# Two output projections and the embedding gate: 512 output channels per product, weights by half of the contraction, one open sum per token tile

## The chip, the cores and the metric

The kernel runs on one core of a Trainium2 chip. The metric is the device time of one execution in microseconds, median of the timed runs: 1736.26 us before the change (three runs, 1733.51 to 1736.67). The engines are called PE (matrix products), PEld (PE's weight loads), DVE (VectorE), ACT (ScalarE), POOL (GpSimd) and SP (which issues most DMAs).

## The reference, cut to what matters

Two transformer-like blocks on 512 tokens of 1024 channels. The three products that the change touches are `w_out` (block 1), `w_out_2` and `w_ple_gate_2` (block 2), each 512 x 1024 times 1024 x 1024:

```
merged = sigmoid(g_attn) * a + sigmoid(g_conv) * s
x = x + g1 * einsum('btd,de->bte', merged, w_out)            # block 1
...
hx2 = modulate(rmsnorm(x, norm2_g), sh2, sc2)
logits = hx2 @ w_router; affinity = softmax(logits)          # top 64 tokens of each of 16 experts
x = x + g2 * experts(...)                                    # 16 experts, three 1024 x 1024 matrices each
...
x = x + m @ w_out_2                                          # block 2
x = x + sigmoid(rmsnorm(x) @ w_ple_gate_2) * (p @ w_ple_2)   # embedding gate
out = rmsnorm(x) * final_g
```

## The kernel before, in words

Every large product is done in float32r in three parts (`mm3`: high times high, high times low, low times high; both operands are split beforehand into a high part, on ACT, and the rest, on DVE). Weights come through the class `Weights` in the order of use: a chunk of 8 x 128 rows and 256 columns is loaded by SP into tag `wr` (two buffers) and split into `wh` and `wl` (two buffers each). Loading chunk i+2 is queued when the split of chunk i begins.

The three products concerned have tokens on the output's partitions (`gemm_tc`): the token tile of the activations (128 x 128) is stationary and 256 columns of the weights move. For 512 output columns the kernel takes two chunks at once, and goes through the four token tiles one after the other: 2 chunks x 8 steps of the contraction x 3 products for a tile, then that tile's sum is complete and its follow-up work is issued. There are two such passes (512 columns each) per product, so 2 x 4 x 48 = 384 products of 256 columns for each of the three.

The order of all engines is the order in which the Python code issues instructions; each engine works through its own queue in that order. Follow-up work is placed with `hooks` at numbered steps of a tile's products.

- First projection (`gemm_x1`, activations `mg`): after a tile, `post_x1` multiplies by the gate and adds x (DVE, two passes); one tile later `half_T` transposes the rows on PE, copies them and sums their squares on ACT, and in the second pass computes the norm on DVE and POOL; `half_mm` multiplies by the router and computes the softmax (a row of small DVE operations `lg`, `mx`, `aff` around one ACT exponential); `router_aff(t)` transposes tile t's affinities. After the last tile come `router_aff(2)`, `half_T(3, 1)`, `half_mm(3, 1)` and `router_aff(3)`, and then the choice of the top 64, a chain on DVE alone. `eload(tags)` loads the next pieces of the experts' weights into the buffers of the tags named; a piece that has been used calls `eload` with its own tag for the next one, so the first list of tags sets which buffers the pieces of all experts use. At the end of the experts the buffers of tag `wr` go to the first two chunks of block 2.
- Second projection (`post_x3`, activations `m2`): DVE adds the tile to the residual rows `acc`, ACT sums its squares. `norm3(t)` (DVE, POOL power, two DVE passes) makes the normalized rows `x3r`, `put_x3(t)` transposes them (eight PE transposes) and splits them into `x4` (two ACT copies `x4h`, two DVE subtractions `x4l`).
- Embedding gate (activations `x4`): `post_x4` is a sigmoid on ACT, a multiplication and an addition on DVE, a sum of squares on ACT. In the second pass `finish(t)` follows: DVE sum, POOL power, a scaling on DVE of one half and on ACT of the other, and the output's DMAs. The last tile is cut in two pieces of 256 columns.

Of the kernel before, what the change touches and what calls it, by code (L numbers as in the profile page):

```python
# [35 lines left out]
def _constants():  # L36
    """Tables that follow from the shapes alone."""
# [25 lines left out]
def tile_two_blocks(ctx: ExitStack, tc: tile.TileContext, a, out):  # L63
# [41 lines left out]
    # ------------------------------------------------------------------ first loads  # L105
# [78 lines left out]
    # ------------------------------------------------------------------ weights  # L184
# [3 lines left out]
    def warm(n):  # L188
        """products with zeros that keep TensorE's clock up where it would wait for others"""
# [3 lines left out]

    class Weights:
        """Chunks of 256 columns in the order of use: loaded ahead, split exactly into two float32r parts."""

        def __init__(self, specs, allocs=None):
            self.allocs = {} if allocs is None else allocs
# [12 lines left out]
        def begin(self):  # L211
            """the next chunk to be split, after those taken as they are"""
# [10 lines left out]
            if kind in self.allocs:  # L223
                hi, lo = self.allocs[kind](sh)
            else:
                hi = wp.tile([128] + sh, F32R, name="wh", tag="wh")
                lo = wp.tile([128] + sh, F32R, name="wl", tag="wl")
# [4 lines left out]
        def steps(self, i, n=4, lo_engine=None):  # L232
            """split of chunk i (or of the next one that is to be split) in 2 n steps, of ScalarE and VectorE in turn"""
# [31 lines left out]
    class Split:  # L265
        """[128, k, n] as two float32r parts, in buffers of 8 KiB"""
# [23 lines left out]
    def gemm_ct(ps, w, m, xs, nk=KT):  # L290
        """ps[ch, tok] = w[:, m-th 128 columns].T @ xs"""
# [6 lines left out]
    def gemm_tc(ps, w, t, xs, nk=KT):  # L298
        """ps[tok, ch] = xs[:, t-th 128 tokens].T @ w"""
# [62 lines left out]
    # ------------------------------------------------------------------ modulation, norms of x and ctx  # L362
# [38 lines left out]
    def unit(t0, between=lambda: None):  # L401
        """rows of two tiles over their root mean square"""
# [24 lines left out]
    specs += [(w_o1, 0), (w_o1, 256, "b2"), (w_o1, 512), (w_o1, 768, "b2")]  # L427
    wallocs = {}
    W = Weights(specs, wallocs)
# [54 lines left out]
    # keys and values, their products by parts of the contraction as these become known: several sums  # L484
    # are open in a bank, and a product with zeros starts them all
# [107 lines left out]
    def rope(ps, t0):  # L593
        """rotary embedding: [128 tokens, 2 tiles, 4 heads * 64] in PSUM -> [128, 2, 4, 64] in SBUF"""
# [15 lines left out]
    # ------------------------------------------------------------------ keys and values  # L610
# [44 lines left out]
    # steps of a chunk before the split of the next one begins  # L655
# [35 lines left out]
    def ct_chunk(xs, post, hooks=None):  # L691
        """256 channels [ch, tok], two PSUM tiles, each passed to post(m, psum)"""
# [11 lines left out]

    def mod256(n, pool):
        """columns 2048 + 256 n of the modulation"""
# [41 lines left out]
            # columns of the scores in PSUM: own keys before the context's, after them in the last block  # L748
# [105 lines left out]
    # ------------------------------------------------------------------ gated merge  # L854
# [16 lines left out]
    def spread(dst, cols_, tmp_):  # L871
        """columns [128, 8] as a row of 1024 on every partition"""
# [23 lines left out]
    wallocs["b2"] = lambda sh: (big2("wbh", sh, F32R), big2("wbl", sh, F32R))  # L896
# [4 lines left out]
    for j in range(4):  # L901
# [15 lines left out]
        for q, (xs, post) in enumerate(((hx, gate), (os_, proj_a), (hx, gate), (ys_, proj_c))):  # L917
# [7 lines left out]
            if j == 3 and q == 3:  # L925
                i0 = ci[0] + 1
                hooks = {14: [lambda: W.split(i0 + 1)]}
# [3 lines left out]
    # ------------------------------------------------------------------ output projection, router  # L931
# [17 lines left out]
    def router_prep():  # L949
        """the shift's part of the logits on every partition; the gain goes into the weights"""  # L950
# [16 lines left out]
    def post_x1(t, s_, pv):  # L967
        """x + gate * projection"""
# [42 lines left out]
    # the last pair's by halves of the columns, the very last rows in smaller pieces  # L1011
# [55 lines left out]
    def gemm_x1(t, n, ws, hooks):  # L1067
# [4 lines left out]
        for c in range(2):  # L1072
            p_ = bank() if cut or not c else p_
            for _ in gemm_tc(p_[:, c * 256:c * 256 + 256], ws[c], t, mg):
                for h in hooks.get(st, ()):
                    h()
# [810 lines left out]
```

## Time and profile before

| what | value |
|---|---|
| timed runs | 1733.51, 1736.26, 1736.67 us |
| span of the profiled execution, first to last instruction | 1732.3 us |
| PE busy | 1689.4 us (98%) |
| DVE, ACT, POOL busy | 893.1, 590.8, 65.9 us |
| mean granted clock of PE | 0.994 |
| first projection, first to last product | 585.3 to 644.1 us |
| second projection | 1628.4 to about 1676 us |
| embedding gate, first product to the end | 1676.9 to 1732.3 us |

The page lists the profiled execution by its span alone; the median of the timed runs is 3.96 us above that span. "Busy" on PE includes the time in which one product overlaps the next, so the distance from start to start of two products, not the duration of one, tells what one more costs.

### The profile page before, as it was taken

How to read it: one execution, taken by the hardware profiler on the slowest of the kernel's cores; microseconds unless marked ns; L12 is line 12 of the kernel's file. 1: busy time of each engine (PE TensorE's matmuls, PEld its weight loads, DVE VectorE, ACT ScalarE, POOL GpSimd, SP SyncE). 2: the span in 40 equal slices, each digit the busy share in tenths (PEclk: the TensorE clock that was granted, in tenths of full speed). 3: DMA queues.
4: the chain of work that ended last, by engine and by line, in shares of the span. 5: the costliest groups of instructions: out<-in, count | busy, mean ns of one | idle time of the engine just before them, and what ended most of it. 6: DMA issues, size and time to landing. Idle time of an engine off the chain costs nothing.

```text
span 1732.3 us, 23047 instructions
## 1 busy us (share of the span) xinstructions
PE 1689.4 (98%) x9500; PEld 1214.4 (70%) x9500; DVE 893.1 (52%) x1646; ACT 590.8 (34%) x1133; POOL 65.9 (4%) x68
## 2 busy tenths in 40 slices
PE   8999999999999999999999999979999999999998
PEld 5987777777778895443444344347898888877898
DVE  4655565565433433112211221276889999955544
ACT  5454545445322322110111011142435443354333
POOL 2000000000000000000000000040000010000000
PEclk9999999999999999999999999999999999999999
DMA  9243333331222668999999999942332222233431
GB/s 335 90 137 98 98 98 98 119 120 55 97 86 92 223 272 325 361 402 409 409 409 409 409 409 409 400 135 74 97 98 81 90 94 86 88 122 98 131 113 49
DMA packets 176217, 334.56 MB, mean 193 GB/s; under 512 B 6925, under 2 KB 120370, under 8 KB 175856
## 3 DMA queue, kind: packets, MB, share of 16 engines
q1 hardware_dynamic: 173712, 328.50, 52.2%
q0 software_dynamic: 1024, 2.37, 0.4%
q10 hardware_dynamic: 1376, 2.23, 0.4%
q8 instruction: 74, 1.21, 0.3%
q14 instruction: 31, 0.25, 0.0%
HBM read 328.88 MB, written 4.19 MB: 192 GB/s over the span
## 4 chain that ended last, share of the span: by engine, by line
PE 91%; DVE 5%; DMA 2%; ACT 1%; issue 1%; SPq 0%; POOL 0%; POOLq 0%; ACTq 0%; DVEq 0%
PE pb L286 15%; PE pb L287 15%; PE pb L288 15%; PE pu L1204 6%; PE py L1204 6%; PE pg L1168 4%; PE po L806 2%; PE pT L798 2%; PE pb L379 1%; PE s L767 1%; PE pg L1225 1%; DMA wr<-w_in 1%; PE pq L286 1%; PE pq L288 1%; PE pq L287 1%
## 5 line engine op out<-in xcount | busy, mean ns | idle before, releaser
L245 DVE TENSOR_TENSOR wl<-wr,wh 128x512 fp32r<-128x512 f32 x316 | 226.0, 732 | 120.7 <-ACT wh L247 120.7
L247 ACT ACTIVATE wh<-wr 128x512 fp32r<-128x512 f32 x320 | 183.6, 620 | 89.2 <-PE pb L287 63.7
L1559 DVE SCALAR_TENSOR_TENSOR co<-cin,cols,co 128x512 f32<-128x512 f32 x240 | 188.5, 785 | 4.1
L286 PE MATMUL pb<-h2h,wh 128*128 128x512 f32 x448 | 177.3, 396 | 0.0
L287 PE MATMUL pb<-h2l,wh 128*128 128x512 f32 x448 | 174.8, 390 | 0.0
L288 PE MATMUL pb<-h2h,wl 128*128 128x512 f32 x448 | 174.6, 390 | 0.0
L286 PE MATMUL pb<-hxh,wh 128*128 128x512 f32 x320 | 130.3, 407 | 0.0
L288 PE MATMUL pb<-hxh,wl 128*128 128x512 f32 x320 | 125.4, 392 | 0.0
L287 PE MATMUL pb<-hxl,wh 128*128 128x512 f32 x320 | 125.3, 391 | 0.0
L1204 PE MATMUL pu<-ew,xe 128*64 128x512 f32 x512 | 114.8, 595 | 0.0
L1204 PE MATMUL py<-ew,hb 128*64 128x512 f32 x440 | 101.0, 597 | 0.0
L286 PEld LDWEIGHTS pb<-h2h,wh 128*128 128x128 f32 x448 | 84.4, 188 | 19.6 <-issue 2.2
L288 PEld LDWEIGHTS pb<-h2h,wl 128*128 128x128 f32 x448 | 84.2, 188 | 17.9
L287 PEld LDWEIGHTS pb<-h2l,wh 128*128 128x128 f32 x448 | 84.3, 188 | 17.3 <-issue 0.5
L1239 DVE SCALAR_TENSOR_TENSOR yt<-py,gt__5984,g2b 128x512 f32<-128x512 f32 x15 | 10.6, 747 | 144.8 <-PE py L1204 138.3
L773 DVE CUSTOM_DVE_ANT_0 P<-s,cst,sink 128x512 f32<-128x512 f32 (+1 forms) x64 | 52.2, 816 | 57.9 <-PE s L770 57.9
L1204 PEld LDWEIGHTS pu<-ew,xe 128*64 128x64 f32 x512 | 35.3, 137 | 66.0 <-issue 65.4
L1171 ACT ACTIVATE xe<-pg,modc,ga 128x128 f32<-128x128 f32 x64 | 25.9, 454 | 147.8 <-PE pg L1168 147.8
L1168 PEld LDWEIGHTS pg<-Gs,xr 128*128 128x128 f32 x512 | 61.1, 196 | 21.5 <-issue 19.5
L777 ACT ACTIVATE P<-P,m 128x512 f32<-128x512 f32 (+1 forms) x64 | 49.8, 777 | 75.3 <-DVE m L776 70.3
L288 PEld LDWEIGHTS pb<-hxh,wl 128*128 128x128 f32 x320 | 60.0, 188 | 13.3
L286 PEld LDWEIGHTS pb<-hxh,wh 128*128 128x128 f32 x320 | 60.2, 188 | 12.4 <-issue 3.2
(457 smaller groups left out, 3294.6 us busy)
## 6 DMA issues: line engine op xcount, KB each, us to landing
ew<-w_exp_gate SPq DMA_DIRECT2D x64, 1024.0 KB, 17.3
ew<-w_exp_up SPq DMA_DIRECT2D x64, 1024.0 KB, 14.1
ew<-w_exp_down SPq DMA_DIRECT2D x59, 1024.0 KB, 16.1
wr<-w_in SPq DMA_DIRECT2D x58, 1024.0 KB, 5.7
wr<-w_mod SPq DMA_DIRECT2D x16, 1024.0 KB, 5.2
wm<-w_mod SPq DMA_DIRECT2D x8, 1024.0 KB, 12.6
wr<-w_out SPq DMA_DIRECT2D x8, 1024.0 KB, 5.3
wr<-w_proj_attn SPq DMA_DIRECT2D x4, 1024.0 KB, 5.1
```

What stands on the lines that cost most here:

```text
L245: (lo_engine or DVE).tensor_tensor(lo[:, ks], raw[:, ks], hi[:, ks].bitcast(F32), op=OP.subtract)
L247: ACT.activation(hi[:, ks], raw[:, ks], AF.Copy)
L286: PE.matmul(ps, ah, bh, start=first, stop=False)
L287: PE.matmul(ps, ah, bl, start=False, stop=False)
L288: PE.matmul(ps, al, bh, start=False, stop=last)
L773: DVE.tensor_tensor_reduce(p_[:, :n], s2[:, self.s0:self.s0 + n], self.mask, 1.0, sink8[:, 4 * g + i:4 * g + i + 1], op0=OP.add, op1=OP.ma ...
L777: ACT.activation(p_[:, :n], p_[:, :n], AF.Exp, bias=m4[:, i:i + 1], scale=0.125, accum_out=sm[:, i:i + 1])
L798: PE.transpose(p_[:, i, :], self.P[i][:, kk * 128:kk * 128 + 128], ident)
L806: PE.matmul(po[64 * h:64 * h + 64], V[:, vi, g * 64:g * 64 + 64], last[:, :, h, :], start=(kk == 1), stop=(kk == nk), tile_position=(0, 64 ...
L1168: PE.matmul(p_[:, d], xrow(t, ds), Gs[p][:, t], start=(t == 0), stop=(t == NT - 1))
L1204: PE.matmul(ps[64 * e:64 * e + 64, n], lhs(k, e), tiles[e][kk][:, n * 512:n * 512 + 512], start=(k == 0), stop=(k == KT - 1), tile_positio ...
L1559: DVE.scalar_tensor_tensor(co[ct], cin[ct][:, k:k + 512], ctap(k, ct), co[ct], op0=OP.mult, op1=OP.add)
```

## The change

The three products keep their activations stationary, but 512 columns of the weights move at once. A chunk of weights is now 4 x 128 rows (half of the contraction) by 512 columns, the same bytes. A new function `tc_half` goes through all four token tiles with one chunk: with the first half of the contraction it opens one sum (one PSUM bank) for each tile, with the second half it completes them one after the other and calls the follow-up work. Only one chunk is in use at a time, so its successor is split during it in the ordinary buffers, and the additional split buffers (`b2`, `mx`) go. In the second pass of the first projection and of the gate the last tile is still cut in two pieces of 256 columns, now with a bank each from the start. The follow-up work is moved to other steps, and the list of tags of the experts' first pieces is ordered differently. The change also drops all comments.

```diff
+    def halves(w):
+        return [(w[512 * h:512 * h + 512], 512 * n) for n in range(2) for h in range(2)]
...
-                raw = wp.tile([128, k, 256], F32, name="wr", tag="wr")
-                SP.dma_start(out=raw, in_=w[:, c0:c0 + 256].rearrange("(k p) n -> p k n", p=128))
+                n = 2048 // k
+                raw = wp.tile([128, k, n], F32, name="wr", tag="wr")
+                SP.dma_start(out=raw, in_=w[:, c0:c0 + n].rearrange("(k p) n -> p k n", p=128))
...
+    def tc_half(xs, h, ps, post, hooks=None, cut=False):
+        i, w = nextw()
+        nxt = W.steps(i + 1)
+        hooks = hooks or {}
+        for t in range(NT):
+            pieces = 2 if cut and t == NT - 1 else 1
+            if not h:
+                ps[t] = [bank() for c in range(pieces)]
+            ts = slice(t * 128, t * 128 + 128)
+            for c in range(pieces):
+                cs = slice(c * 256, c * 256 + 256) if pieces > 1 else slice(0, 512)
+                p_ = ps[t][c][:, 0:cs.stop - cs.start]
+                for kk in range(4):
+                    k = 4 * h + kk
+                    mm3(p_, xs.hi(k, ts), xs.lo(k, ts), w[0][:, kk, cs], w[1][:, kk, cs], k == 0,
+                        k == KT - 1)
+                    if not c:
+                        ahead(nxt, 4 * t + kk)
+                        for f in hooks.get(4 * t + kk, ()):
+                            f()
+                        yield
+                if h:
+                    post(t, cs, p_)
...
     for n in range(2):
-        ws = [nextw()[1], nextw()[1]]
...
-                hooks = {3: [lambda: half_T(lt, ln)], 5: [lambda: half_mm(lt, ln)]}
-                if n and t > 1:
-                    hooks[1] = [lambda: router_aff(t - 2)]
...
-                            lambda: eload("B B B B wr wr B2 B2 wh wl wh wl B2 B2 B2 B")]
...
+            hooks[eload_at + 1] = [lambda: eload("B B B B B2 B2 B2 B2")]
+        else:
+            hooks[0] = [lambda: half_mm(NT - 2, 0)]
+            hooks[1] = [lambda: half_T(NT - 1, 0)]
+            hooks[3] = [lambda: half_mm(NT - 1, 0)]
+            hooks[9] = [pw_T]
+        run(tc_half(mg, 0, ps, None, hooks, n == 1))
+        hooks = {}
+        for t in range(NT - 1):
+            hooks[4 * t + 7] = [lambda t=t: half_T(t, n)]
+            hooks.setdefault(4 * t + 10, []).append(lambda t=t: half_mm(t, n))
+        if n:
+            hooks[0] = [lambda: eload("wr wr wh wl")]
+            hooks[13] = [lambda: router_aff(0)]
+        run(tc_half(mg, 1, ps, lambda t, cs, p_: post_x1(t, slice(512 * n + cs.start, 512 * n + cs.stop), p_),
+                    hooks, n == 1))
+    eload("wh wl B2 B")
+    half_mm(NT - 2, 1)
+    router_aff(1)
...
-    for t in range(NT):
-        hooks = {}
-        if t == 1:
-            hooks[1] = [lambda: W.split(ci[0])]
-        if t == 2:
-            hooks[1] = [lambda: norm3(0)]
-        if t == 3:
-            hooks = {1: [lambda: norm3(1)], 3: [lambda: put_x3(0)], 4: [lambda: W.split(ci[0] + 1)]}
-        post_x3(t, 1, walk(gemm_n(m2, 1, t, ws), hooks))
-    norm3(2)
+    for n in range(2):
+        ps = {}
+        run(tc_half(m2, 0, ps, None))
         hooks = {}
+        if n:
+            x4 = Split("x4", 512, mix((1, 1, 0, 0)))
+            hooks = {6: [lambda: norm3(0)], 10: [lambda: norm3(1)], 12: [lambda: put_x3(0)], 14: [lambda: norm3(2)]}
+        run(tc_half(m2, 1, ps, lambda t, cs, p_: post_x3(n, t, cs, p_), hooks))
...
-    put_x3(1)
     norm3(3)
...
+    for n in range(2):
+        ps = {}
+        hooks = {} if n else {0: [lambda: put_x3(1)], 3: [lambda: put_x3(2)], 7: [lambda: put_x3(3)]}
+        run(tc_half(x4, 0, ps, None, hooks, n == 1))
+        run(tc_half(x4, 1, ps, post_x4b if n else post_x4a, None, n == 1))
```

`post_x4b` calls `finish(0)` and `finish(1)` right after those tiles' squares and `finish(2)` after the sigmoid of the last tile's first piece, as the loop before did.

Two places in the queues, before and after. The first is DVE where the second projection ends and the gate begins. `L1771` (after: `L1772`) adds a tile's sum to the rows `acc`, `rr` and `x3r` are `norm3`, `x4l` is the subtraction in `put_x3`, two for each token tile. Before:

```order
L1771 TENSOR_TENSOR acc_6269<-pb,acc_6269 128x512
L1755 SCALAR_TENSOR_TENSOR rr<-sq_11684 128x1
L1759 SCALAR_TENSOR_TENSOR x3r<-acc_6269,rr,g1bple_norm_g_11680 128x512 x2
L1771 TENSOR_TENSOR acc_6270<-pb,acc_6270 128x512
L1755 SCALAR_TENSOR_TENSOR rr<-sq_11684 128x1
L1759 SCALAR_TENSOR_TENSOR x3r<-acc_6269,rr,g1bple_norm_g_11680 128x512 x2
L1768 TENSOR_TENSOR x4l_11933<-pT,x4h_11931 128x4x128
L1768 TENSOR_TENSOR x4l_11934<-pT,x4h_11932 128x4x128
L245 TENSOR_TENSOR wxl<-wr,wxh 128x512 x4
L1771 TENSOR_TENSOR acc_6270<-pb,acc_6270 128x512
L1755 SCALAR_TENSOR_TENSOR rr<-sq_11684 128x1
L1759 SCALAR_TENSOR_TENSOR x3r<-acc_6270,rr,g1bple_norm_g_11680 128x512 x2
```

After the change, from the same addition (tile 2's) to the subtractions of tile 1:

```order
L1772 TENSOR_TENSOR acc_6102<-pb,acc_6102 128x512
L1769 TENSOR_TENSOR x4l_11721<-pT,x4h_11719 128x4x128
L1769 TENSOR_TENSOR x4l_11722<-pT,x4h_11720 128x4x128
L1756 SCALAR_TENSOR_TENSOR rr<-sq_11516 128x1
L1760 SCALAR_TENSOR_TENSOR x3r<-acc_6102,rr,g1bple_norm_g_11512 128x512 x2
L1772 TENSOR_TENSOR acc_6102<-pb,acc_6102 128x512
L1756 SCALAR_TENSOR_TENSOR rr<-sq_11516 128x1
L1760 SCALAR_TENSOR_TENSOR x3r<-acc_6102,rr,g1bple_norm_g_11512 128x512 x2
L1769 TENSOR_TENSOR x4l_11721<-pT,x4h_11719 128x4x128
L1769 TENSOR_TENSOR x4l_11722<-pT,x4h_11720 128x4x128
```

Tile 2's norm now stands ahead of the last tile's addition, and the last tile's norm ahead of the two subtractions of tile 1, which stood ahead of it before.

The second place is PE where the first projection ends. `pl` is `half_mm`, `pt` is `router_aff`, `pT` is `half_T`, `pw` is other work. Before:

```order
L288 MATMUL pb<-wbh,mgl_4070 128x256
L989 MATMUL pl<-wr__233,xT 128x16 x4
L286 MATMUL pb<-wbh,mgh_4071 128x256
...
L288 MATMUL pb<-wbh,mgl_4073 128x256
L1005 MATMUL pt<-cst,aff 32x128
L978 MATMUL pT<-cst,xr_5205 128x128 x4
L1059 MATMUL pw<-wpl,pk 128x512
L989 MATMUL pl<-wr__233,xT 128x16 x4
```

After:

```order
L1001 MATMUL pT<-cst,xr_5193 128x128 x4
L288 MATMUL pb<-wh,mgh_4071 128x256
...
L290 MATMUL pb<-wh,mgl_4073 128x256
L1012 MATMUL pl<-wr__233,xT 128x16 x4
L1028 MATMUL pt<-cst,aff 32x128 x2
L1001 MATMUL pT<-cst,xr_5193 128x128 x4
L1082 MATMUL pw<-wpl,pk 128x512
L1012 MATMUL pl<-wr__233,xT 128x16 x4
```

`half_mm(2, 1)` stood 12 products ahead of the projection's last one and now stands behind it, with `router_aff(1)` and `router_aff(2)` between it and `half_T(3, 1)`.

## Rows read from the trace of the kernel before

**Rows 1.** the page's chain that ended last: share of the span by engine

```profile
PE 91%; DVE 5%; DMA 2%; ACT 1%; issue 1%; SPq 0%; POOL 0%; POOLq 0%; ACTq 0%; DVEq 0%
```

**Rows 2.** timeline of PE, products 512 columns wide (start us, us, engine, line)

```profile
1609.82 0.39 PE L288 MATMUL pb<-ybh,wl 128*128 128x512 f32 x1
...
1622.51 0.39 PE L287 MATMUL pb<-ybl,wh 128*128 128x512 f32 x1
```

**Rows 3.** timeline of PE, products 256 columns wide, second projection

```profile
1639.73 0.28 PE L287 MATMUL pb<-wxl,m2h 128*128 128x256 f32 x1
...
1646.45 0.28 PE L286 MATMUL pb<-wh,m2h 128*128 128x256 f32 x1
```

**Rows 4.** timeline of PE at the second projection's start

```profile
1631.03 0.28 PE L287 MATMUL pb<-wl,m2h 128*128 128x256 f32 x1
...
1632.07 0.39 PE L287 MATMUL pb<-wxl,m2h 128*128 128x256 f32 x1
```

**Rows 5.** timelines where the gate begins; in brackets idle before, and releaser

```profile
1664.54 0.15 DVE L1755 SCALAR_TENSOR_TENSOR rr<-sq 128x1 f32<-128x1 f32 x1
1665.38 1.42 DVE L1759 SCALAR_TENSOR_TENSOR x3r<-acc,rr,g1bple_norm_g 128x512 f32<-128x512 f32 x2 [0.69 <-POOL rr L177]
...
1669.69 0.69 DVE L1771 TENSOR_TENSOR acc<-pb,acc 128x512 f32<-128x512 f32 x1 [2.89 <-PE pb L288]
...
1670.47 0.63 ACT L1772 ACTIVATE jk<-acc 128x512 f32<-128x512 f32 x1 [5.04 <-DVE rr L1755]
...
1676.12 1.04 PE L1766 MATMUL pT<-cst,x3r 128*128 128x128 f32 x8
```

**Rows 6.** timeline of ACT and DVE at the gate's last tiles

```profile
1713.53 0.60 ACT L1805 ACTIVATE t<-pb 128x512 f32<-128x512 f32 x1 [1.38 <-PE pb L288]
...
1717.19 0.72 ACT L1829 ACTIVATE acc<-acc,rr 128x512 f32<-128x512 f32 x1 [0.85 <-POOL rr L177]
1719.29 0.60 ACT L1805 ACTIVATE t<-pb 128x512 f32<-128x512 f32 x1 [1.38 <-PE pb L288]
...
1723.61 0.42 DVE L1809 TENSOR_TENSOR t<-pw,t 128x256 f32<-128x256 f32 x1
...
1725.86 0.42 DVE L1810 TENSOR_TENSOR acc<-t,acc 128x256 f32<-128x256 f32 x1
...
1727.68 0.75 DVE L1827 SCALAR_TENSOR_TENSOR acc<-acc,rr,g2bfinal_g 128x512 f32<-128x512 f32 x1 [0.66 <-POOL rr L177]
```

**Rows 7.** timeline of DVE and PE at the first projection's end

```profile
641.60 0.16 DVE L983 TENSOR_TENSOR s<-sq 128x1 f32<-128x1 f32 x1 [2.83 <-ACT jk L981]
...
642.66 0.16 DVE L994 TENSOR_TENSOR lg<-lg,pl 128x16 f32<-128x16 f32 x1
...
644.28 0.23 DVE L1001 TENSOR_SCALAR aff<-lg,mx 128x16 f32<-128x16 f32 x1
...
643.79 0.28 PE L288 MATMUL pb<-wbh,mgl 128*128 128x256 f32 x1
...
645.37 0.44 PE L978 MATMUL pT<-cst,xr 128*128 128x128 f32 x2 [0.29 <-DVE xr L970]
```

**Rows 8.** timeline where the experts end and block 2 begins

```profile
1132.82 3.65 PE L1339 MATMUL py<-ew,hb 128*64 128x512 f32 x16 [0.85 <-DVE yt L1239]
...
1134.78 24.41 SPq L207 DMA_DIRECT2D wr<-w_in  x3
...
1139.17 3.65 PE L1339 MATMUL py<-ew,hb 128*64 128x512 f32 x16
...
1141.89 1.13 ACT L247 ACTIVATE wh<-wr 128x512 fp32r<-128x512 f32 x2
...
1146.70 0.63 ACT L1257 ACTIVATE sqx<-acc 128x512 f32<-128x512 f32 x1 [3.68 <-DVE acc L1227]
...
1150.82 1.27 PE L1393 MATMUL pT<-cst,hr 128*128 128x128 f32 x8 [3.44 <-ACT hr L1431]
```

**Rows 9.** tile wr, 1130 to 1162 us: issue to landing

```profile
DMA to landing us min/median/max: 6.3/6.3/6.3
```

More of the change, by code (lines that the diff above doesn't have):

```diff
@@ L222, in begin @@
             sh = list(raw.shape[1:])
[L223 to L227, printed above, removed]
+            hi = wp.tile([128] + sh, F32R, name="wh", tag="wh")
+            lo = wp.tile([128] + sh, F32R, name="wl", tag="wl")
             self.parts[i] = (hi, lo)
@@ L426, in tile_two_blocks @@
         specs += [(w_in, 4608 + 256 * j), (w_pa1, 256 * j), (w_in, 5632 + 256 * j), (w_pc1, 256 * j)]
-    specs += [(w_o1, 0), (w_o1, 256, "b2"), (w_o1, 512), (w_o1, 768, "b2")]
-    wallocs = {}
-    W = Weights(specs, wallocs)
+    specs += halves(w_o1)
+    W = Weights(specs)
     ci = [0]
@@ L1065, in pw_tile @@
         yield
[L1067 to L1101 removed]
+    eload_at = 6
+    for n in range(2):
+        ps = {}
+        hooks = {}
+        if not n:
+            hooks[2] = [router_prep]
+            hooks[eload_at] = [pw_load]
+            hooks[eload_at + 1] = [lambda: eload("B B B B B2 B2 B2 B2")]
[5 more added lines that the diff above has]
+        run(tc_half(mg, 0, ps, None, hooks, n == 1))
+        hooks = {}
+        for t in range(NT - 1):
[9 more added lines that the diff above has]
+    router_aff(1)
     xe = big("xe", [2, KT, 128])
@@ L1375, in tile_two_blocks @@
     for n in ("w_out_2", "w_ple_gate_2"):
-        specs += [(a[n][0], 256 * j) + (("mx",) if j % 2 else ()) for j in range(4)]
-    W = Weights(specs, {"mx": lambda sh: (big3("wxh", sh, F32R), big("wxl", sh, F32R))})
+        specs += halves(a[n][0])
+    W = Weights(specs)
     ci[0] = 0
@@ L1736, in tile_two_blocks @@
     x4h = {}
-    def gemm_n(xs, n, t, ws):
-        p_ = bank()
-        for c in range(2):
-            yield from gemm_tc(p_[:, c * 256:c * 256 + 256], ws[c], t, xs)
-        yield p_
-    def take2():
-        i0 = ci[0]
-        ci[0] += 2
-        ws = [W.get(i0), W.get(i0 + 1)]
-        W.load(i0 + 3)
-        return ws
     x3r = {}
@@ L1814, in square_x4 @@
                        accum_out=sq3[:, t, i:i + 1])
-    def post_x4(t, n, p_):
-        t_ = gate_x4(half(n), p_)
-        add_x4(t, half(n), t_)
-        square_x4(t, half(n), n)
     def finish(t):
@@ L1830, in finish, with post_x4a, post_x4b @@
         SP.dma_start(out=out_d[:, t, half(0)], in_=arow(t, half(0)))
-    ws = take2()
-    for t in range(NT):
-        hooks = {}
-        if t == 0:
-            hooks[4] = [lambda: put_x3(2)]
-        if t == 1:
-            hooks[2] = [lambda: put_x3(3)]
-            hooks[4] = [lambda: W.split(ci[0])]
-        if t == 2:
-            hooks[4] = [lambda: W.split(ci[0] + 1)]
-        post_x4(t, 0, walk(gemm_n(x4, 0, t, ws), hooks))
-        DVE.tensor_mul(arow(t, half(0)), arow(t, half(0)), fgb[:, half(0)])
-    ws = take2()
-    for t in range(NT):
-        if t < NT - 1:
-            post_x4(t, 1, walk(gemm_n(x4, 1, t, ws), {}))
+    def post_x4a(t, cs, p_):
+        t_ = gate_x4(cs, p_)
+        add_x4(t, cs, t_)
+        square_x4(t, cs, 0)
+        DVE.tensor_mul(arow(t, cs), arow(t, cs), fgb[:, cs])
+    def post_x4b(t, cs, p_):
+        cs = slice(512 + cs.start, 512 + cs.stop)
+        if cs == half(1):
+            t_ = gate_x4(cs, p_)
+            add_x4(t, cs, t_)
+            square_x4(t, cs, 1)
             if t < NT - 2:
                 finish(t)
-            continue
-        cs = [slice(512, 768), slice(768, 1024)]
-        ps = [bank()[:, 0:256] for c in range(2)]
-        run(gemm_tc(ps[0], ws[0], t, x4))
-        t0 = gate_x4(cs[0], ps[0])
-        finish(t - 1)
-        add_x4(t, cs[0], t0)
-        run(gemm_tc(ps[1], ws[1], t, x4))
-        t1 = gate_x4(cs[1], ps[1])
-        square_x4(t, cs[0], 1)
-        add_x4(t, cs[1], t1)
-        square_x4(t, cs[1], 2)
-        finish(t)
+        elif cs.stop < D:
+            t_ = gate_x4(cs, p_)
+            finish(t - 1)
+            add_x4(t, cs, t_)
+        else:
+            t_ = gate_x4(cs, p_)
+            square_x4(t, slice(512, 768), 1)
+            add_x4(t, cs, t_)
+            square_x4(t, cs, 2)
+            finish(t)
+    for n in range(2):
+        ps = {}
+        hooks = {} if n else {0: [lambda: put_x3(1)], 3: [lambda: put_x3(2)], 7: [lambda: put_x3(3)]}
+        run(tc_half(x4, 0, ps, None, hooks, n == 1))
+        run(tc_half(x4, 1, ps, post_x4b if n else post_x4a, None, n == 1))
 _INS = ['x', 'c', 'ctx', 'c_ctx', 'w_mod', 'b_mod', 'norm1_g', 'w_in', 'attn_sink', 'conv_w', 'w_proj_attn',
```

41 lines of the change are left out of this document (2 added, 39 removed).

## The prediction, made before the changed kernel ran

> **What bounds the kernel now.** I read the chain that ended last first: PE holds 91% of it [rows 1], so elsewhere a microsecond of products saved is a microsecond of time. Then I read PE's timeline inside such a stretch for the distance from start to start, because durations overlap: 56 steps of 512 columns take 12.69 us, 0.2266 each [rows 2]; 56 steps of 256 columns take 6.72 us, 0.1200 each [rows 3]. Last I read DVE and ACT where a projection ends and its successor needs the result, since there PE stops being the bound if a tile's follow-up takes longer than its products.
>
> **Products: what is removed.** One product of 512 columns replaces two of 256: 0.2400 - 0.2266 = 0.0134 us per pair. The second projection has 384 products before and 192 pairs, all joined: 2.57 us. In the first projection and in the gate the cut last tile of the second pass keeps 24 pairs apart (2 halves x 4 steps x 3 parts), which leaves 168: 2.25 us each. That is 7.1 us in all, if PE remains the bound. The stationary side (128 x 128) and the types are those of the products that gave 0.2266, so I take this row, though there the activations move and here the weights. Bounds: 0, if moving 512 columns of weights costs as much as two halves, and 7.1.
>
> The Trainium skill ("TensorE: Matmul & The Clock Gate", section "Back-to-back issue gap") gives the warm distance of isolated products as N/2.4 + 2.5 ns. By it a pair of 256 costs 218.3 ns and one of 512 215.8, an estimate of 2.5 ns gained per pair and 1.3 us in all, where the rows give 13.4 ns and 7.1 us; the trace disagrees (120.0 and 226.6 ns), and the sum goes by the rows.
>
> **A head stall removed.** At the start of the second projection three steps take 1.04 us instead of 0.36 [rows 4], because the last activations and the second chunk's split come late. With half of the contraction in front, the last activations are needed 11 us later and only one chunk has to be ready: 0.68 saved (bounds 0 and 0.68). At the first projection I count 0.4, between the same bounds. Second projection: -2.57 - 0.68 = **-3.2 us**.
>
> **What the order of the sums does.** Before, a tile's sum was completed every 48 x 0.12 = 5.76 us. Now the first half of the contraction completes none, and the second half completes one every 12 x 0.2266 = 2.72 us. Follow-up that fitted into 5.76 us has to fit into 2.72, or it queues. I go through the places.
>
> **First projection, its end.** PE arrives 2.25 + 0.4 = 2.65 us earlier. Behind the last product stood only `router_aff(2)` and `half_T(3, 1)`, whose second pair of transposes began 1.58 us after the last product's start (645.37 - 643.79 [rows 7]). Now `half_mm(2, 1)` and two `router_aff` are in between, and `router_aff(2)` needs the softmax of tile 2. Count from the start H of `half_T(2, 1)`: transposes 0.4, ACT copy, square and its sum 1.4, so DVE's `s` at H + 1.8 (before, DVE idled 2.83 us for the same ACT work [rows 7]); two small operations 0.3; the two pieces of the last tile, four passes of 0.42 to 0.45 us: H + 3.9; the softmax, from 642.66 to 644.51 [rows 7], 1.85: H + 5.8; transposes at H + 6.0. The last product starts at H + 1.85, so the transposes now follow by 4.15 instead of 1.58: +2.6. I add 0.4 because `half_T(2, 1)` itself waits for additions that stand behind tile 1's norm on DVE. Net 2.6 + 0.4 - 2.65 = **+0.3 us** (bounds -1.2, if DVE reaches the softmax before the pieces, and +1.5). What follows is the top-64 chain on DVE, so nothing behind it hides this.
>
> **Loads of the experts.** Sixteen pieces are still queued ahead of the experts, but the last four only at the first projection's end. The experts use twelve others first, which covers it, so I price it at nothing; uncovered it would cost a landing, 6.3 us for a load of this size [rows 9]. But the list of tags repeats: from piece 20 on a piece takes the tag of the piece 15 earlier (the pieces 3, 15 to 18 are not renewed). Tags before, from there: B B B wr wr B2 B2 wh wl wh wl B2 B2 B2 B2; after: B B B B2 B2 B2 B2 wr wr wh wl wh wl B2 B2. The last eight pieces are 188 to 195, two per quarter of the last product. (188 - 20) mod 15 = 3, so `wr` was held by 188 and 189, of the first quarter; now `wr` is at 7 and 8, that is 192 and 193, of the third. The first quarter's products start at 1132.82 and SP issued block 2's first load at 1134.78, 1.96 later; the third quarter starts at 1139.17 [rows 8], so the issue moves to 1141.13, 6.35 us later. Landing took 6.3 us [rows 9]: 1147.4. On ACT two splits of that chunk (at 1141.89, 1.13 us for both) stand ahead of the squares at 1146.70, before which ACT had idled 3.68 [rows 8]. They would now start at 1147.4 and push the squares to about 1148.4; the norm and the rows `hr`, for which PE waits at 1150.82 [rows 8], hang on them. I take **+1.7 us** (bounds 0, if the load lands in the gap, and 6.35, if the whole delay goes through).
>
> **From the second projection to the gate.** Here DVE's queue decides, as the order of the section on the change shows. A norm occupies DVE from 1664.54 to 1666.80, 2.2 us, of which 0.69 is the wait for POOL [rows 5]. Count from the end of tile 0's products in the last quarter. DVE begins norm 0 about 2.6 us later (an addition 0.69, ACT's square 0.8, a split between). Then, in its queue, until the subtraction of tile 1: four norms 8.8, three additions 2.0 [rows 5], a split 0.6, two subtractions of tile 0 1.2, and three waits for ACT squares or copies (0.63 and more each [rows 5]) about 2.6: 15.2, less overlaps of neighbours 0.3. So `x4l` of tile 1 is there at 2.6 + 14.9 + 0.6 = 18.1 us. PE wants it after three tiles 8.2, three groups of eight transposes at 0.87 with the switch behind them (8 in 1.04 [rows 5], the next product overlapping) 2.6, gate tile 0 2.7 and two products 0.45: 14.0. **PE stalls 4.1 us**, where it had none (bounds 0 and 5).
>
> **The end of the gate.** A tile's follow-up from its sigmoid at 1713.53 to the scaling on ACT at 1717.19, behind which the next sigmoid stands in ACT's queue, takes 3.66 + 0.62 = 4.3 us; PE delivered a tile every 5.76 (1713.53 to 1719.29 [rows 6]). With 2.72 per tile, ACT's queue is the bound: sigmoids of tiles 0, 1, 2 at G, G + 4.3, G + 8.6. From tile 2's sigmoid on: 4.32 to the first piece's multiplication (1719.29 to 1723.61), three passes of about 0.42, 1.25, and from the second addition to the end of the last scaling 2.57 (1725.86 to 1728.43 [rows 6]): 8.15. In all 16.75 us from G. And G from the gate's start: 144 products of 512 (32.6), 24 of 256 (2.9), transposes 2.6, stall 4.1, end of the product 0.4: 42.6. Together 59.3 us, where 1676.12 to 1728.43 was 52.3 [rows 5, 6]: **+7.0 us**. The saving of this product is inside that sum and is lost, as ACT waits for nothing of PE at the end.
>
> **Sum.** +0.3 + 1.7 - 3.2 + 7.0 = +5.8 us. Span 1732.3 + 5.8 = 1738.1; the median of the runs lies 3.96 above the span, so 1736.26 + 5.8 = **1742.1 us**, 0.33% more. The remaining edits (chunks of other shape but the same bytes and the same number of split passes, fewer split buffers) I cost at nothing: splits run on ACT and DVE during 10.9 us of products per chunk and take 4 x 0.7 there; without that cover a chunk's split would cost 2.5 us.
>
> **Rivals.** (1) The border is covered: DVE's waits overlap better than I count, and the 4.1 us stall is near 0, or the first projection keeps its 2.65 us. Then +1 to +3: 1737.9 with the stall at 0. For it: three of my waits are estimates; against it: the norms alone are 8.8 us in a stretch of 14.0. (2) PE stays the bound everywhere, the other side: -7.1 - 0.68 - 0.4 and the late load +1.7 = -6.5, 1729.8 us. It needs follow-up of at most 2.72 us per tile, the point from which it decides; for it speaks the 91% of PE [rows 1], against it 4.3 us per tile at the end [rows 6]. (3) The late load goes through whole, 6.35 instead of 1.7: 1746.7. For it: DVE, ACT and POOL all work on that norm, and a delay on one may queue on the others. (4) A 512-column product with weights moving costs as much as two of 256, 0.2400 us: then the pairs gain nothing, 504 of them count (168, 192, 144), 6.8 us more, 1748.9. Against it: the products of rows 2 have the same shape and types. By the formula of the Trainium skill named above, nearly this would hold.
>
> **Chances.** A measurement of this kernel can tell about 0.2%, 3.5 us, from no change. Forecast 0.63, rival 1 0.19, rival 2 0.08, rival 3 0.07, rival 4 0.03. Faster by over 0.2%: 0.08; within: 0.19; slower: 0.63 + 0.07 + 0.03 = 0.73. The forecast alone, with bounds of the stall and of the load mostly in, spans 1739.8 to 1744.8; with rival 1 down to 1736 and part of rival 3, 1736 to 1746.
>
> **What would show it.** Right: distance 0.2266 in all three products; PE idle for `x4h` and `x4l` at the gate's start, some 4 us in all; sigmoids of the gate's last tiles 4.3 us apart with PE long done; the last product of the first projection earlier but `router_aff(2)` waiting some 3 us for `aff`; block 2's first load issued about 2 us after the third quarter's products begin instead of the first's, with its split on ACT just ahead of late squares. Wrong: no idle PE at the gate's start, sigmoids 2.7 us apart, or a span below 1733.

## The result, and the profile after

Four runs of the changed kernel gave 1744.65 us (1744.29 to 1745.13), four of the kernel before beside them 1736.27 (1733.51 to 1736.67). The medians are 8.4 us apart, 1.0048; the ratio on record is 1.0057, 95% interval 1.0044 to 1.0070, which at its middle is 10 us. The profiled executions span 1742.7 and 1732.3 us, 10.4 apart. Of these 2.0 are there before the first projection begins, where both kernels run the same work: its first product starts at 585.3 us in one trace and at 587.3 in the other. Of the 2.0, 1.3 come from 30 to 35 us, where PE's granted clock is 1.00 in the one trace and 0.66 in the other. It is 0.66 there in seven of the ten traces of this study that have the changed first projection, and in none of the three with the old one. So the change does not bring it each time; whether it has a part in it no run shows. I leave the 2.0 out. What remains is 8.35 us, and the traces say where it lies:

| stage, first projection's start as zero | change | forecast |
|---|---|---|
| first projection, router, to the last expert products | +2.5 | +0.3 |
| block 2's late first load, as left at the second projection | +1.7 | +1.7 |
| second projection | -3.4 | -3.2 |
| gate, border included | +7.6 | +7.0 |
| sum | +8.4 | +5.8 |

Two of these lines are flattered by the one trace of the kernel before, whose own clock fell at two places that the change does not touch: 1.6 us at the first gather, in the first line, and 1.1 us in block 2, in the second. Neither stands in the other traces as a rule; both are shown below. Without them the lines would be +4.1 and +2.8, and the sum +11.1, an estimate from the same traces.

The share of PE in the chain that ended last is what it was [rows 1]. In the page of the changed kernel:

```profile
PE 91%; DVE 4%; ACT 2%; issue 1%; DMA 1%; POOL 0%; SPq 0%; POOLq 0%; ACTq 0%; DVEq 0%
```

A share over 1740 us doesn't show 8. The stages do. First the distance of the products, PE's timeline in the second projection (answers to [rows 2, 3]):

```profile
1638.92 0.39 PE L289 MATMUL pb<-wl,m2h 128*128 128x512 f32 x1
...
1652.52 0.39 PE L289 MATMUL pb<-wl,m2h 128*128 128x512 f32 x1
```

60 steps take 13.60 us, 0.2267 each, with the weights moving as with the activations. The saving per pair is real in this projection.

The gate's end, timelines of PE, ACT and DVE (answers to [rows 6]):

```profile
1730.09 0.28 PE L290 MATMUL pb<-wh,x4l 128*128 128x256 f32 x1
...
1722.16 0.60 ACT L1790 ACTIVATE t<-pb 128x512 f32<-128x512 f32 x1 [5.47 <-PE pb L290]
...
1726.44 0.58 ACT L1790 ACTIVATE t<-pb 128x512 f32<-128x512 f32 x1
...
1730.70 0.58 ACT L1790 ACTIVATE t<-pb 128x512 f32<-128x512 f32 x1
...
1738.06 0.75 DVE L1807 SCALAR_TENSOR_TENSOR acc<-acc,rr,g2bfinal_g 128x512 f32<-128x512 f32 x1 [0.66 <-POOL rr L177]
```

The sigmoids stand 4.28 and 4.26 us apart, and only the first has a wait for PE beside it. PE's last product starts at 1730.09, when tile 2's sigmoid has not yet begun. From tile 0's sigmoid to the end of the last scaling it is 16.6 us.

The border to the gate (where [rows 5] stand), PE's waits from 1615 to 1740 us (in total, times, longest). The view has no more than these two, and before the change neither was there:

```profile
PE pb L288 <- ACT x4h L1768: 1.9, 2, 1.6
PE pb L290 <- DVE x4l L1769: 1.6, 1, 1.6
```

At the second projection's start, where [rows 4] show 0.68 us lost, PE now waits for nothing.

The end of the experts (answers to [rows 8]):

```profile
1143.72 3.65 PE L1353 MATMUL py<-ew,hb 128*64 128x512 f32 x16
...
1145.68 0.99 SPq L212 DMA_DIRECT2D wr<-w_in  x2
...
1152.26 1.15 ACT L249 ACTIVATE wh<-wr 128x512 fp32r<-128x512 f32 x2 [5.74 <-issue]
1153.31 0.61 ACT L1271 ACTIVATE sqx<-acc 128x512 f32<-128x512 f32 x1
...
1158.16 1.97 PE L1407 MATMUL pT<-cst,hr 128*128 128x128 f32 x8 [6.24 <-ACT hr L1445]
```

SP issues the load 1.96 us after the third quarter's products begin, ACT stands 5.74 us, and the squares that stood ready follow its split. The view names no releaser for that; the split needs what the load brings, and it begins 6.58 us after the issue, where a landing took 6.3 [rows 9]. Block 2's first transposes start 14.44 us behind the third quarter, 2.8 more than the 11.65 of before. On the way from there to the second projection the changed kernel is 1.1 us shorter, 476.5 us for 477.6. That difference comes at one place, the 12 us that begin 19.2 us behind the first transposes' start. Windows (length, PE busy, PEld, DVE, ACT, POOL, granted clock, DMA share, GB/s) for the kernel before and the changed one show it in the granted clock, 0.72 and 0.86:

```profile
1170.00:1182.00 12.00, 8.35 (x36) 7.73 (x37) 8.66 (x18) 3.16 (x6) 1.84 (x1) 0.72 0.29 88
1177.34:1189.34 12.00, 8.36 (x41) 7.64 (x42) 9.32 (x19) 3.81 (x7) 1.82 (x1) 0.86 0.29 87
```

What I had not seen coming is at the first projection's end (answers to [rows 7]), timelines of PE and DVE:

```profile
643.92 0.28 PE L290 MATMUL pb<-wh,mgl 128*128 128x256 f32 x1
...
648.31 0.28 PE L1028 MATMUL pt<-cst,aff 128*32 128x128 f32 x1 [3.12 <-DVE aff L1024]
648.43 0.60 PE L1001 MATMUL pT<-cst,xr 128*128 128x128 f32 x4
648.87 1.62 PE L1082 MATMUL pw<-wpl,pk 128*128 128x512 f32 x2
...
651.85 2.06 PE L1082 MATMUL pw<-wpl,pk 128*128 128x512 f32 x2
...
654.65 0.68 DVE L1143 MAX8 m<-affT 32x8 f32<-32x512 f32 x1
...
654.67 14.62 PE L1082 MATMUL pw<-wpl,pk 128*128 128x512 f32 x28 [0.37 <-DVE affT L1029]
...
671.47 0.29 DVE L1162 COPY post<-pt 128x128 f32<-128x128 f32 x1 [2.50 <-PE pt L1161]
```

and the same stretch in windows of the same columns:

```profile
645.00:648.00 3.00, 0.20 (x2) 0.00 (x0) 2.28 (x9) 0.40 (x2) 0.54 (x1) 1.00 0.81 288
648.00:652.00 4.00, 3.69 (x16) 2.75 (x17) 1.01 (x5) 1.21 (x3) 0.54 (x1) 0.65 1.03 422
652.00:656.00 4.00, 3.63 (x6) 1.24 (x6) 2.72 (x10) 1.00 (x3) 0.00 (x0) 0.50 1.02 407
656.00:660.00 4.00, 4.00 (x6) 1.56 (x6) 3.79 (x10) 0.60 (x1) 0.00 (x0) 0.57 0.20 75
660.00:665.00 5.00, 5.00 (x13) 2.26 (x12) 4.79 (x10) 1.79 (x3) 0.00 (x0) 1.00 0.41 154
```

Before the change, the last products of p with its weights, and DVE's copy of the transposed `work`:

```profile
649.85 12.18 PE L1059 MATMUL pw<-wpl,pk 128*128 128x512 f32 x28
665.26 0.29 DVE L1148 COPY post<-pt 128x128 f32<-128x128 f32 x1 [0.59 <-PE pt L1147]
```

PE stands 3.12 us for `aff`, as forecast. Then its granted clock is 0.50 to 0.65, mostly the lower of its two levels, 1.2 and not 2.4 GHz, until about 659. The products of p with its weights, which stand in PE's queue ahead of the transposes of `work`, run long: two take 2.06 us where two took 1.10 before, and 28 take 14.62 instead of 12.18. So DVE, done with the top-64 chain, waits 2.50 us for those transposes, where it waited 0.59 before.

### The profile page after: what moved, and what is told of

Its sections match the earlier page's. It is cut to its first block, busy times and chain, and to the rows that moved or that the text cites. A ratio compares the mean times of both kernels' runs of the same rounds, so it can differ in the third digit from the quotient of the medians.

```text
span 1742.7 us, 21975 instructions
## 1 busy us (share of the span) xinstructions
PE 1689.9 (97%) x8972; PEld 1189.4 (68%) x8972; DVE 893.3 (51%) x1646; ACT 590.0 (34%) x1133; POOL 66.0 (4%) x68
## 3 DMA queue, kind: packets, MB, share of 16 engines
q8 instruction: 70, 1.15, 0.3%
## 4 chain that ended last, share of the span: by engine, by line
PE 91%; DVE 4%; ACT 2%; issue 1%; DMA 1%; POOL 0%; SPq 0%; POOLq 0%; ACTq 0%; DVEq 0%
PE pb L288 15%; PE pb L290 15%; PE pb L289 15%; PE pu L1218 6%; PE py L1218 6%; PE pg L1182 4%; PE po L833 2%; PE pT L825 2%; PE pb L381 1%; PE s L794 1%; PE pg L1239 1%; PE pw L1082 1%; PE pq L288 1%; PE pq L289 1%; PE pq L290 1%
## 5 line engine op out<-in xcount | busy, mean ns | idle before, releaser
L247 DVE TENSOR_TENSOR wl<-wr,wh 128x512 fp32r<-128x512 f32 x340 | 241.7, 727 | 143.0 <-ACT wh L249 143.0
L249 ACT ACTIVATE wh<-wr 128x512 fp32r<-128x512 f32 x344 | 197.5, 620 | 123.1 <-PE pb L289 63.7
```

The source lines that it names most:

```text
L247: (lo_engine or DVE).tensor_tensor(lo[:, ks], raw[:, ks], hi[:, ks].bitcast(F32), op=OP.subtract)
L249: ACT.activation(hi[:, ks], raw[:, ks], AF.Copy)
```

## The experiments

The microseconds expected stand on the scale of a kernel before at 1736.3. Other chips gave it at about 1734, so ratios to the runs beside each are compared, and the traces from the first projection's start.

**One part alone, first projection.** Block 1 of the changed kernel, the second projection and the gate of before:

```diff
...
-        specs += halves(a[n][0])
+        specs += [(a[n][0], 256 * j) + (("mx",) if j % 2 else ()) for j in range(4)]
...
```

> Only the first projection by halves, with its own order of the experts' slots; the second projection and the gate as before. If the stages add up as the two traces show them (the first projection +2.5 us at the end of the experts, the late first load of block 2 +1.7), it stands 4.2 us above the kernel before, near 1740.5. The rival, that the first projection costs what the prediction said (+0.3) and the rest of the loss is in the second projection and the gate, gives +2.0, near 1738.3.

1.0035 (1.0022 to 1.0048). The 1.0024 of adding stages is in the interval, the 1.0012 of the rival outside. In its trace PE stands 3.12 us for `aff` again, and the clock is 0.69, 0.84 and 0.78 in the three windows of 5 us from 645 on. The missed size is in block 1, the first projection and the late load together.

**One part alone, second projection.** The reverse, block 1 and gate of before:

```diff
...
-    ws = take2()
-    for t in range(NT):
-        post_x3(t, 0, walk(gemm_n(m2, 0, t, ws), {1: [lambda: W.split(ci[0] + 1)]} if t == 1 else {}))
+    for n in range(2):
+        ps = {}
+        run(tc_half(m2, 0, ps, None))
...
+        run(tc_half(m2, 1, ps, lambda t, cs, p_: post_x3(n, t, cs, p_), hooks))
...
```

> Only the second projection by halves; the first projection and the gate as before. The products should gain the 3.5 us that the trace of the changed kernel shows from the first to the last of them. The gate's tiles then ask for their normalised rows 5.4 us apart and not 2.7, so that of the stalls at its start only those of tile 0 should be left, some 2 us: 1734.8. If the stalls at the border are as long as in the changed kernel (4.6 us with the first wait), the gain is gone: 1737.

0.9994 (0.9985 to 1.0003): no gain that can be measured; the 0.9991 of 1734.8 us is in the interval, the 1.0004 of 1737 just outside. In the trace the projection is 3.4 us shorter and the stretch from its last product to the gate's last 3.0 us longer (51.7, before 48.7). PE's waits there:

```profile
PE pb L291 <- ACT x4h L1798: 0.7, 1, 0.7
PE pb L293 <- DVE x4l L1799: 0.4, 2, 0.2
PE pb L292 <- DVE wxl L250: 0.3, 1, 0.3
```

Only 1.4 us carry a name; counted from start to start, the same four places cost about 2.1 us more than their products need. The 2 us expected was about right for these places, but the stretch lost 3.0: in the trace most of the gain is handed back at the next stage even when that keeps its old form.

**The stand filled.** Does the stand itself cost, or what it does to the clock? Products of ones fill it:

```diff
     router_aff(1)
+    p_ = bank("pt", (128,))
+    for i in range(13):
+        PE.matmul(p_, one, one, start=(i == 0), stop=(i == 12))
```

> The changed kernel with 13 float32 products of 128 x 128 ones (26 passes at 0.122 us, 3.2 us) between the transpose of tile 1's affinities and that of tile 2's, where TensorE stands for 3.12 us. If the fall of the granted clock behind that stand is the cause of the late experts, the clock stays at 1.0 from 645 to 660, the top-64 chain begins about 1.2 us earlier and the one-hot matrices about 3 us earlier; the first gather may then fall to the low clock as it did before the change, which would give 1.6 us back: 1741.6 to 1743.2. If the late softmax of tile 2 is the whole cause, the products fill a wait that ends when it did: 1744.7.

PE's timeline:

```profile
644.64 3.06 PE L1118 MATMUL pt<-one 128*128 128x128 f32 x26
647.91 0.28 PE L1028 MATMUL pt<-cst,aff 128*32 128x128 f32 x1 [0.21 <-DVE aff L1024]
...
650.23 1.10 PE L1082 MATMUL pw<-wpl,pk 128*128 128x512 f32 x2
...
652.62 12.18 PE L1082 MATMUL pw<-wpl,pk 128*128 128x512 f32 x28
```

`aff` comes no sooner, but the products of p take 12.18 us instead of 14.62. From the transposes of the last tile to the top-64 chain it is 5.10 us instead of 6.22, from there to the one-hot matrices 15.22 instead of 17.14: 3.0 us together, as the clock theory said; the rival gave none. The ratio was 1.0046 (1.0034 to 1.0059), which alone does not tell the two apart: 1.0031 to 1.0040 was expected, 1.0048 by the rival. The profiled execution lost 1.6 us at the gate, where the clock fell behind the stalls of the border:

```profile
1685.00:1690.00 5.00, 5.00 (x20) 4.06 (x20) 3.31 (x6) 1.45 (x4) 0.00 (x0) 0.66 0.00 0
```

**The late load undone.** The slots of pieces 177 and 178 get no further piece:

```diff
-                if i not in (3, 15, 16, 17, 18):
+                if i not in (3, 15, 16, 17, 18, 177, 178):
```

> The changed kernel with the two weight slots left free once pieces 177 and 178 of the experts' weights are used, so that the last four pieces go to other slots and block 2's first load waits for no piece of the last expert pair. If the late load is worth what the traces show at the end of block 2's first stages, the time falls by 1.7 us, to 1743.0, and block 2's first transposes stand 2.8 us earlier against the last down products. If the squares and not the load are the limit there, nothing changes: 1744.7.

1.0046 (1.0034 to 1.0059), with the expected 1.0039 and the rival's 1.0048 both inside; the trace decides. SP's and PE's timelines:

```profile
1126.91 34.86 SPq L212 DMA_DIRECT2D wr<-w_in  x3
...
1153.40 1.97 PE L1407 MATMUL pT<-cst,hr 128*128 128x128 f32 x8 [3.44 <-ACT hr L1445]
```

The load goes out ahead of the last down products, PE waits 3.44 us for `hr` as before the change, and its transposes follow the third quarter by 11.64 us, not 14.44: the 2.8 is that load's. At the second projection's start 2.7 us of the changed kernel's 4.2 are gone, 1.0 more than the forecast of the term. The load now goes out earlier than before the change, too, but that adds nothing: the wait for `hr` is the same 3.44 us.

**Another order in the gate's last pass.** A routine `tc_seq` runs (tile, columns, half) in a given order:

```diff
...
+    EARLY = [(0, WHOLE, 0), (1, WHOLE, 0), (0, WHOLE, 1), (1, WHOLE, 1)]
+    TILES = EARLY + [(2, WHOLE, 0), (2, WHOLE, 1)] + [(3, c, h) for c in (LEFT, RIGHT) for h in range(2)]
...
+        if n:
+            run(tc_seq(x4, TILES, post_x4b))
...
```

> The changed kernel with the order of the halves in the gate's last pass altered: first halves of tiles 0 and 1, their second halves, then tile 2 and the two pieces of tile 3 each through the whole contraction. The sums then end 8.2, 10.9, 16.3 and 21.8 us into the pass and not 2.7 us apart at its end, so that three of the four chains of 4.26 us lie beside products. If those chains are the tail, the last scaling follows the last product by some 3.5 us and not by 8.1: a gain of 4.3 us, 1740.4. The rival: the last weight chunk, now wanted 5.4 us into the pass, is split too late and TensorE waits for it some 2.5 us: 1742.9.

1.0048 (1.0036 to 1.0061): the rival. The last scaling now starts 3.0 us behind the last product's start and not 8.0, yet the end moves by 0.9 only, as PE came 4.1 us later:

```profile
1715.26 0.50 PE L288 MATMUL pb<-wh,x4h 128*128 128x512 f32 x1 [1.45 <-ACT wh L249]
1716.06 0.50 PE L289 MATMUL pb<-wl,x4h 128*128 128x512 f32 x1 [0.30 <-DVE wl L247]
...
1718.03 0.63 PE L289 MATMUL pb<-wl,x4h 128*128 128x512 f32 x1
1718.45 0.63 PE L290 MATMUL pb<-wh,x4l 128*128 128x512 f32 x1
```

The split of the last chunk, wanted 5.4 us into the pass, stood in ACT's queue behind tile 3's follow-up: 1.8 us. Then the distance of products is 0.43 and not 0.23 us for some 3 us, and the granted clock of 1715 to 1720 is 0.70. The Trainium skill ("TensorE: Matmul & The Clock Gate", section "Wait — 56ns, not 53.3ns?") gives N / 1.2 GHz from start to start on the cold array, 426.7 ns at 512 columns; here the trace agrees (0.42 to 0.43).

**The border reordered too.** The second projection's last pass ends tiles 0 and 1 first (`EARLY`), then 2 and 3 by halves, and the norms move forward:

```diff
...
+        run(tc_seq(m2, PAIRS, lambda t, cs, p_: post_x3(n, t, cs, p_),
+                   {(3, 1): [lambda: norm3(0)], (4, 1): [lambda: norm3(1)], (5, 1): [lambda: put_x3(0)],
+                    (6, 2): [lambda: put_x3(1)], (7, 1): [lambda: norm3(2)]}))
...
```

> As the run before it, and the second projection's last pass with tiles 0 and 1 finished first, then tiles 2 and 3 by halves, so that the norms of two tiles lie beside products. If the stalls at the border are the norms', TensorE's waits for x4h and x4l (3.5 us) and the first wait of 1.1 us go, but for one of about a microsecond: another 3.5 us below the run with the gate alone, 1736.9. The rival: the gate's first chunk, whose buffer comes free only 5.4 us before the border, is late in its place, and nothing more is gained.

1.0021 (1.0013 to 1.0030). The waits for `x4h` and `x4l` are gone. One of 1.77 us for the split of the gate's first chunk took their place, which is the rival in part, but from the run before to this one the trace's end moves 5.2 us. Not all of that is the border's: counted from start to start, its stalls shrink by some 2 us. Some 3 come in the gate's last pass, where PE no longer waits 1.45 us for the last chunk's split (0.05 and 0.31 us are left) and the clock stays at 1.00, where it was 0.70.

**The first projection in that order,** with tile 2's router sums between the two pieces of tile 3:

```diff
...
+                 (5, 3): [lambda: router_aff(0)], (7, 0): [lambda: router_aff(1)], (7, 2): [lambda: half_T(2, 1)],
+                 (8, 1): [lambda: half_mm(2, 1)]}
+        run(tc_seq(mg, TILES, post, hooks))
+    eload("wh wl wh wl B2 B")
...
```

> The changed kernel with the first projection's last pass in that order, tile 2's router sums between the two pieces of tile 3 and its softmax ahead of the last piece on VectorE. TensorE then does not stand 3.1 us. If that stand, with the low clock behind it, is what the first projection lost, the top-64 chain begins some 4 us earlier against the start of the projection, and the experts 4 to 6 us earlier; a low clock at the first gather may take 1.6 of it: 1741. If the low clock comes from elsewhere, the top-64 chain gains its 1.1 to 2 us and the projected tiles of p stay slow: 1743.

1.0029 (1.0018 to 1.0041), with the expected 1.0027 and the rival's 1.0039 both inside; the trace decides. The stand is gone, and with it the low clock:

```profile
645.95 1.02 PE L1120 MATMUL pw<-wpl,pk 128*128 128x512 f32 x2
...
650.16 12.18 PE L1120 MATMUL pw<-wpl,pk 128*128 128x512 f32 x28
```

Against the projection's start the top-64 chain begins 4.1 us earlier than in the changed kernel, and the one-hot matrices 6.0.

**Everything together,** with the two free slots, and more products of ones at the first gather:

```diff
...
-    warm2(8)
+    warm2(12)
...
-    warm2(4)
+    warm2(7)
...
```

> The three orders together, with the two free weight slots, and 12 and 7 products of ones in place of 8 and 4 around the transposes before the first gather, which keep TensorE busy there. If the gains add (4.3 at the end, 3.5 at the border, 4.2 at the router, 1.7 at block 2, 1.6 at the gather), it stands near 1730, some 5 us below the kernel before. If one undoes another, or the clock falls in a new place, it stands at the kernel before or above.

0.9967 (0.9955 to 0.9980), 1728.5 against 1733.6 us: faster than either kernel. The gains nearly add. How much of them the kernel before would have had from the same orders, without the 512 columns, no run shows.

**Three more beside each other.** First the same, with the follow-up of the gate's first pass on tile 3 behind the last chunk's split:

```diff
...
+            run(tc_seq(x4, TILES, post_x4b, {(1, 3): late}))
...
```

> The three orders together, and the follow-up work of the gate's first pass on its last tile put behind the split of the last weight chunk, which ScalarE and VectorE did only after it. In the run with the gate's order alone TensorE waited 1.45 and 0.30 us there and then ran 3.2 us at the low clock; with the three orders 2.1 us. If the place in ScalarE's queue is the cause, the wait goes and the time is 2 us below that of the three orders: 1726.5 against 1734 for the kernel before. If the buffer of the chunk, free only at the end of the pass, is the limit, half of it stays: 1727.5.

0.9967 (0.9954 to 0.9979), no different. The wait for that split went, but with the three orders it had been only 0.30 us, and the trace's end comes 1.0 us sooner behind the first projection's start; the 1.77 was the split of the gate's first chunk. I had put both at one place.

Then the kernel before with nothing but those products of ones:

> The kernel before with 12 and 7 products of ones in place of 8 and 4 around the transposes ahead of the first gather, and nothing else. In its profile TensorE stands 1.01 and 0.84 us there, the clock is 0.76 from 665 to 670 us, and the first 32 gather products take 5.44 us against 3.81 in the changed kernel, whose clock stayed up. If the stands cause the fall, every execution should now take 3.8 us there, 1.6 below the profile, and the time falls by 0 to 1.6 us, as often as the fall came in the runs before. If the fall has another cause, nothing changes.

0.9999 (0.9990 to 1.0008). First gather, in the kernel before, and then with the added products:

```profile
667.15 5.44 PE L1168 MATMUL pg<-Gs,xr 128*128 128x128 f32 x32 [0.84 <-DVE Gs L1159]
```

```profile
666.69 3.81 PE L1168 MATMUL pg<-Gs,xr 128*128 128x128 f32 x32 [0.17 <-DVE Gs L1159]
```

The low clock is gone there, yet the time shows nothing. The run with the second projection alone left that place as it was and has 3.81 us too, and so have all other traces but that one of the kernel before: there the clock falls in some executions only, and how often is open. In the execution with the added products the clock fell elsewhere, to 0.57 from 1002 to 1006 us, among the experts, which cost it 1.5 us.

Last, the changed kernel once more:

> The changed kernel once more, beside the other runs on one chip: 1.0057 of the kernel before. If TensorE's fall to the low clock after the stand of 3.12 us belongs to the change, the profile shows it again at the end of the first projection (two products of 512 columns at 0.43 us each and not 0.23); if it was chance, the experts begin some 3 us earlier.

1.0063 (1.0050 to 1.0075). The stand of 3.12 us is there, and the products of p take 14.06 us. So it is in each of the six traces that keep the stand unfilled, 13.91 to 14.89. At the gate this execution fell to 0.69 from 1690 to 1695, behind the same stalls that left the first profile's clock at 1.00.

## Where the prediction was right, and which step failed

The direction and the places held. The size did not: +5.8 us forecast, +8.4 between the medians, about 10 by the ratio on record and 11 by the repeated run. The step that failed is what follows the stand at the first projection's end: it was taken at its old durations, so the low clock behind the stand was put at nothing. A second term, the late load, was too small and came out right by luck.

**Products and head stall.** 0.2267 per product and -3.4 us in the second projection: right. Rival 4 is out. The formula that the prediction cites from the Trainium skill does not hold for these products; by it the pairs would have given 1.3 us in all.

**First projection, forecast +0.3, measured +2.5.** This is the term that failed. From first to last product it gained 1.9 us, not 2.65. Counted from start to start, its products with `mg` take 46.6 us where they took 47.8, so they gave 1.15; the other 0.7 of the 1.9 is that eight small products of `half_mm(2, 1)` moved behind the last one. The transposes of the last tile start 4.51 us behind the last product (648.43 - 643.92), for which the prediction counted 4.15 where it had been 1.58. So far +1.0, inside its bounds. It then took what follows at its old durations. But the stand that it foresaw put PE at the low clock: 1.2 us more to the top-64 chain, 1.9 more to the one-hot matrices. The first gather, slow in the one profile of before, was not slow here, -1.6; that is chance of that profile and no gain of the change, as the run with the second projection alone shows. Sum -1.9 + 2.9 + 1.2 + 1.9 - 1.6 = +2.5, and +4.1 without the chance. The filled stand gives the clock's 3.0 us back; the reordered projection removes stand and low clock together.

**Late load, forecast +1.7, measured +2.8.** The issue came 1.96 us into the third quarter, where the prediction put it. At block 2's start it costs 2.8, and free slots give 2.7 back. That 1.7 are left at the second projection is luck: the other 1.1 is the longer low clock in block 2 of the one profile of before (0.72 against 0.86 over 12 us), not something that the late load earns. The stretch from block 2's first transposes to the second projection takes 476.4 us in the kernel before with the added products of ones and 476.5 with the free slots, neither with a late load, and 477.7 with the reordered first projection, which has it. Rival 3, the whole delay of 6.35 us, is out.

**Border and gate, forecast +7.0, measured +7.6.** Stalls of 3.5 us by name, 4.2 counted from start to start, forecast 4.1; 16.6 us from tile 0's sigmoid, forecast 16.75. The two reorderings show that this is the order of the sums and not the 512 columns: with both, the last scaling starts 97.0 us behind the second projection's start instead of 103.4, and before the change 99.3.

**Rivals.** Rival 1 (border covered) and rival 2 (PE the bound everywhere) fell to the same rows. The reordered kernel, at -0.33%, comes near rival 2's 1729.8, with free slots and added products of ones besides, and shows what it would have needed: sums that end far enough apart for their follow-up.

## What to carry to other kernels

Splitting the contraction halves the weights that are held, but it brings all sums to their end together, and the follow-up of a tile then has half the time; where that is longer than a tile's products, an order that ends some tiles early keeps both gains. A stand of the matrix engine should be priced with what runs behind it at the low clock, about once more its own length here, and a few products of ones in it are worth trying. When slots are renewed in a fixed round, look which of them the next stage waits for.

## What the chip showed that I had not expected

The low clock came after a stand of 3.12 us at the router, in each of the six executions that had it unfilled, and after 1.45 and 0.30 us close together in the gate. It doesn't come each time: the border's stalls of 1.56, 0.30 and 1.65 us left the clock at 1.00 in one execution of the changed kernel and took it to 0.69 in another, 1.6 us longer from the gate's first product to its last. It was so in two of the six traces with that border. Elsewhere, in work that is the same in all kernels, the clock fell in some executions and not in others: from 30 to 35 us in seven of thirteen traces (1.3 us), at the first gather in one (1.6), among the experts in one (1.5), and longer than in the others at block 2's start in five (1.1). Runs of one kernel differ by as much (1743.7 to 1746.8 us in the last one), and a comparison of two single traces, as in the table above, carries these spells in its terms.
